# The values of the mLSTM mixer, split where they are made and stored as two parts

## The chip, the cores and the metric

One core of one Trainium2 chip runs the kernel. The metric is device time in microseconds of one launch, taken over several runs of the same program; the profile is one further execution of it. Every engine name is that of the profile: PE multiplies matrices, DVE, ACT and POOL work elementwise, SP and ACT issue the transfers of this kernel.

## The reference

One inference step of a trunk with two layers: a gMLP mixer (A) and an xLSTM mLSTM mixer (B), over 1024 frames of a prompt and 8 running streams of 16 frames each. All is fp32. What bears on the change is mixer B, for which the reference has, cut down:

```python
proj = xn @ w_in
xm, z = proj[..., :E], proj[..., E:]                  # E = 2048
xc = silu(causal_conv(xm))                            # 4 taps
q, k, v = blockdiag(xc, wq), blockdiag(xc, wk), blockdiag(xm, wv)
gates = concat(q, k, v) @ w_gates + b_gates           # ig, lf for each of 4 heads
# for each head (width 512) and chunk, with the state C (512 x 512) and n (512):
s   = (q @ k.T) * w_intra
num = s @ v + w_inter * (q @ C)
den = s.sum(-1) + w_inter * (q @ n)
h   = num / maximum(abs(den), exp(-m))
C   = decay * C + (w * k).T @ v
n   = decay * n + (w * k).sum(time)
# h: normalised per head, + skip * xc, * silu(z), @ w_out, + residual
```

The prompt starts from C = 0; each of the 8 sample streams has a state C for each head (1 MB each), which is read, updated and written back.

## The kernel before

The tokens stand in nine tiles of 128: eight of the prompt (n = 0 to 7) and one (n = 8) with the 8 x 16 sample frames. An fp32 product is made of three matmuls of rounded parts: `split` (L89, L90) gives a high part (a cast, on ACT) and a low part (source minus high part, on DVE, or on POOL where the call names `G`), and `mm3` multiplies high by high, high by low and low by high. All matmuls are issued by one wrapper (L58), so PE's rows in the profile all have that line and are told apart by their tiles. PE's order is that of a written list; the order of the other engines is made by a scheduler, and a tile that is given out again makes its next writer wait for its last reader.

The stages, with their place in the profiled execution: mixer A to about 840 us; the feature stage of mixer B (about 850 to 1145 us), 48 steps of some 6 us, one for each of 16 blocks of 128 features and 3 batches of 3 token tiles; the gates and the z projection (1145 to 1405 us), beside which the first sample streams begin; the loop over 32 units, one for each head h and prompt tile n, and 4 riders (the sample tile of each head), with 22 sample streams among them (1405 to 1945 us); a short tail.

In a feature step `values` multiplies the inputs of the batch by block-diagonal weights into a PSUM tile of 128 x 3 x 136, copies the 3 x 128 values to an SBUF tile `st` (ACT, L777), adds the other columns to the gates (DVE, L778) and stores `st` to the scratch tensor `vb_d` of the head (a transfer issued by ACT, L779). `st` has 5 buffers, which the skip product `sk` (L780 to L782) and the z steps (L857 to L859) use too. `keys` makes queries and keys and stores them to `q_d` and `k_d` (L798). The inputs of the next feature go through a convolution on DVE (L755, L758), a silu on ACT (L760) and a split of two halves (`xc`, L89 and L90).

At the end of the feature stage the gates are gathered (`rA`, DVE, L887), `bgc` and `m0T` (L892, L894) are loaded, and the states of the first sample streams (`c`, L1111, 512 KB a transfer) are requested on the same queue, SP's.

`load_qkv` (L1016 to L1042) loads what a unit needs by transfers on SP's queue: `qT`, `kT`, `sk`, `zz`, the values `vv` (256 KB, L1031) and the decay weights `cw` (L1037). In the loop `mask` adds `cw` to a mask into `dd` (DVE, L1211), `prep_k` and `prep_s` scale and split keys and scores, `prep_v` (L1240 to L1247) splits `vv` into `va`, the operand tile of the values, with the high part on ACT and the low part on POOL, `scale_q` (L1252) and `prep_q` do the same for the queries, and `settle` updates the state `Cst` (L1278) and splits it into `Ch` and `Cl`, whose low part is made in four pieces, some on DVE and some on POOL. `va` has three buffers that take turns; two more columns of each hold ones and zeros, set once. `numerator` and `update` use the parts of `va` as operands of PE. After the numerator come the normalising operations (L1318 to L1330), the gate products (L1361, L1363) and the output projection, whose sums are added to the residual on DVE (L1380).

A head's sample tile is prepared by the class `Dec`: `keys` turns the keys to tokens, weights them (`kw`, L1082), splits keys and values (L1084, L1085; the low parts on POOL) and stores six pieces of them to the scratch tensor `st_d` (L1088), from which each stream loads its operand `sk` (L1108); `normaliser` updates n by a matmul over 512 columns and an operation on 8 partitions (`nn`, L1097).

Of the kernel before, what the change touches and what calls it, by code (L numbers as in the profile page):

```python
# [8 lines left out]
F32 = mybir.dt.float32  # L9
# [61 lines left out]
def trunk_kernel(ctx: ExitStack, tc: tile.TileContext, ins: dict, outs: list):  # L71
# [56 lines left out]
    vb_d = [dram.tile([NT * P, DH], F32, name=f"vb_d{h}") for h in range(H)]  # L128
# [577 lines left out]
    class Feature:  # L706
# [60 lines left out]
        def values(self, b):  # L767
# [8 lines left out]
            st = bw.tile([P, 3, P], F32, name="st", bufs=5)  # L776
            A.copy(out=st, in_=pvv[:, :, :P])  # L777
            V.tensor_tensor(out=gtok[:, 3 * b:3 * b + 3], in0=gtok[:, 3 * b:3 * b + 3], in1=pvv[:, :, P:], op=ALU.add)  # L778
            A.dma_start(out=vb_d[h].rearrange("(n p) e -> p n e", p=P)[:, 3 * b:3 * b + 3, fs], in_=st)  # L779
            sk = bw.tile([P, BT], F32, name="st", bufs=5)  # L780
# [67 lines left out]
    def z_steps():  # L848
        for f in range(NF):
# [3 lines left out]
            for b in range(NB):  # L853
# [3 lines left out]
                st = zs.tile([P, BT], F32, name="st", bufs=5 if zs is bw else 2)  # L857
# [129 lines left out]
    dec8 = const.tile([SB, H], F32, name="dec8")  # L987
    selh = gt.tile([H, H, P], F32, name="selh")
    V.tensor_copy(out=selh, in_=ident[:H, :H].unsqueeze(2).to_broadcast([H, H, P]))
    tpd, tp8 = (ps.tile([P, DH], F32, name="sm") for _ in range(2))  # L990
    for h in range(H):
        T.matmul(tpd[:, 16 * h:16 * h + 16], selh[:, h], de16, start=True, stop=True)
    T.transpose(tp8[:SB, :H], de16[:, 8:16], ident[:H, :H])
    V.tensor_copy(out=decB.rearrange("p h c -> p (h c)"), in_=tpd[:, :16 * H])
    V.tensor_copy(out=dec8, in_=tp8[:SB, :H])
# [22 lines left out]
    def load_qkv(pool, h, n, want, prev=None, bufs=None):  # L1018
# [10 lines left out]
        if "v" in want:  # L1029
            t = pool.tile([P, DH], F32, name="vv")  # L1030
            l = S.dma_start(out=t, in_=vb_d[h][ts, :])  # L1031
            if prev is not None:
                after(l, prev)
            got["v"] = t
# [17 lines left out]
    class Dec:  # L1052


        def __init__(self, h, prev):
# [4 lines left out]
            kv = self.kv = rawp.tile([P, 2, DH], F32, name="raw")  # L1060
            loads = (S.dma_start(out=kv[:, 0].rearrange("p (c t) -> p c t", c=DC), in_=k_d[h].rearrange("(c p) t -> p c t", p=P)[:, :, 8 * P:]),
                     S.dma_start(out=kv[:, 1], in_=vb_d[h][8 * P:, :]))
# [3 lines left out]
            self.nn = dw.tile([SB, DH], F32, name="nn")  # L1066
            S.dma_start(out=self.nn, in_=ins["state_mlstm_n"][0, :, h])
# [5 lines left out]
        def keys(self):  # L1073
# [6 lines left out]
            kp = k_tokens(self.kv[:, 0].rearrange("p (c t) -> p c t", c=DC), ps, "sm")  # L1080
            kw = self.kw = rawp.tile([P, DH], F32, name="raw")
            A.activation(out=kw, in_=kp, func=AF.Copy, scale=tok[:, 8, 1, h:h + 1])  # L1082
            kv = wp.tile([P, 4, DH], F32R, name="w")
            split(kv[:, 0], kv[:, 1], kw, G)  # L1084
            split(kv[:, 2], kv[:, 3], self.kv[:, 1], G)  # L1085
            for r, (kpart, vpart) in enumerate(((0, 2), (0, 3), (1, 2))):
                for q, part in enumerate((kpart, vpart)):
                    S.dma_start(out=f32(st_d[h])[:, r * SL:(r + 1) * SL, q, :], in_=f32(kv)[:, part])  # L1088
# [499 lines left out]
```

## Time and profile before

| | us |
|---|---|
| runs (three) | 1966.57, 1967.85, 1975.25 |
| median | 1967.85 |
| profiled execution, its own time | 1961.52 |
| its span in the trace | 1959.8 |
| busy: PE | 1900.5 (97%) |
| busy: DVE | 1270.3 (65%) |
| busy: ACT | 850.0 (43%) |
| busy: POOL | 621.4 (32%) |
| DMA, mean over the span | 167 GB/s, 328.21 MB |

The profiled execution is 6.33 us below the median of the runs. In the views of the trace a busy time is the union of an engine's instructions; a wait is the idle time of an engine before an instruction, put down to what ended it; the chain is the work that ended last, followed back from the end; PEclk is the clock granted to PE, as a share of 2.4 GHz, so that 1.00 is the upper of its two levels and 0.50 the lower (1.2 GHz). DMA is the mean busy share of the 16 DMA engines.

### The profile page before, as it was taken

The numbers are of one execution on the slowest core, as the hardware profiler recorded it, in microseconds if no ns is written. First come the engines' busy times: TensorE is split into PE (matmuls) and PEld (weight loads), VectorE is DVE, ScalarE is ACT, GpSimd is POOL, SyncE is SP. The second block draws the span as 40 slices with busy tenths as digits, with TensorE's granted clock in tenths as the row PEclk, the third lists the DMA queues.
The fourth block names the chain that finished last, engine by engine and source line by source line (L and its number), as shares of the span: only waits on it lengthen the run. The fifth ranks groups of instructions, "written<-read, shape, count | busy, mean of one in ns | idle before, by whom it ended". The sixth has DMA issues, their size and how long they took to land.

```text
span 1959.8 us, 32037 instructions
## 1 busy us (share of the span) xinstructions
PE 1900.5 (97%) x11553; PEld 1681.2 (86%) x11553; DVE 1270.3 (65%) x2522; ACT 850.0 (43%) x1727; POOL 621.4 (32%) x637
## 2 busy tenths in 40 slices
PE   7999999999998999989999989999999999999998
PEld 6888999999998788889999959888987787788887
DVE  5822477777776354477667635222498798898897
ACT  5422444444444243455555635112343344344454
POOL 3000244444441000035444401000145435345466
PEclk9999999999999999999999979999999999999999
DMA  6222333333334654335555554687998897775533
GB/s 213 92 92 77 106 98 103 103 103 99 103 98 163 200 170 142 113 99 154 161 162 156 167 152 143 207 259 235 282 306 264 267 284 243 261 239 177 154 122 129
DMA packets 345690, 328.21 MB, mean 167 GB/s; under 512 B 28164, under 2 KB 276948, under 8 KB 345532
## 3 DMA queue, kind: packets, MB, share of 16 engines
q1 hardware_dynamic: 288812, 261.03, 43.3%
q10 hardware_dynamic: 56720, 65.13, 10.6%
q8 instruction: 91, 1.49, 0.3%
q14 instruction: 67, 0.55, 0.1%
HBM read 203.07 MB, written 123.02 MB: 166 GB/s over the span
## 4 chain that ended last, share of the span: by engine, by line
PE 74%; DVE 13%; DMA 7%; ACT 2%; issue 2%; POOL 1%; SPq 1%; ACTq 0%; POOLq 0%; DVEq 0%
PE sm L58 74%; DVE Cst L1278 2%; DMA cw<-cw_d 2%; DVE c L1129 2%; DVE Cl L90 1%; DVE qT L1252 1%; DMA out<-c 1%; DVE raw L1361 1%; DVE bst L1318 1%; DMA c<-in_state_mlstm_C 1%; DMA vv<-vb_d 1%; DMA r<-in_a_w_in 0%; DVE dn L1324 0%; DVE x L1380 0%; DMA st_d<-w 0%
## 5 line engine op out<-in xcount | busy, mean ns | idle before, releaser
L58 PE MATMUL sm<-xh,w 128*128 128x384 f32 x1536 | 410.9, 341 | 4.3 <-DVE w L90 1.5
L58 PEld LDWEIGHTS sm<-xh,w 128*128 128x128 f32 x1536 | 281.5, 189 | 12.8 <-issue 8.2
L58 PE MATMUL sm<-xl,w 128*128 128x384 f32 x768 | 260.4, 339 | 1.1 <-DVE xl L90 1.1
L58 PE MATMUL sm<-Xh,w 128*128 128x288 f32 x1024 | 216.3, 298 | 4.6 <-ACT c L499 4.6
L58 PE MATMUL sm<-w,o 128*128 128x512 f32 x864 | 209.9, 398 | 2.9 <-ACT o L89 1.2
L58 PE MATMUL sm<-w,os 128*128 128x512 f32 x864 | 200.7, 393 | 6.6 <-ACT os L89 6.6
L58 PEld LDWEIGHTS sm<-w,os 128*128 128x128 f32 x864 | 162.9, 190 | 42.8 <-ACT os L89 9.1
L58 PEld LDWEIGHTS sm<-w,o 128*128 128x128 f32 x864 | 159.8, 188 | 41.1 <-ACT hn L1330 1.7
L58 PE MATMUL sm<-w,Xh 128*128 128x512 f32 x576 | 180.2, 394 | 1.8 <-DVE w L90 1.4
L58 PEld LDWEIGHTS sm<-Xh,w 128*128 128x128 f32 x1024 | 168.2, 189 | 5.2 <-ACT c L499 5.0
L90 DVE TENSOR_TENSOR w<-r,w 128x512 fp32r<-128x512 f32 x176 | 136.1, 779 | 50.3 <-ACT w L89 49.8
L58 PE MATMUL sm<-S,w 128*128 128x288 f32 x1152 | 163.8, 297 | 0.0
L90 DVE TENSOR_TENSOR w<-raw,w 128x1024 fp32r<-128x1024 f32 x44 | 56.4, 1281 | 156.8 <-ACT w L89 156.7
L58 PEld LDWEIGHTS sm<-S,w 128*128 128x128 f32 x1152 | 155.1, 188 | 0.8
L58 PE MATMUL sm<-Xl,w 128*128 128x288 f32 x512 | 151.4, 296 | 0.0
L58 PEld LDWEIGHTS sm<-xl,w 128*128 128x128 f32 x768 | 145.1, 189 | 1.3 <-DVE xl L90 1.3
L89 ACT CAST w<-r 128x512 fp32r<-128x512 f32 x176 | 107.3, 618 | 68.8 <-PE sm L58 29.3
L58 PEld LDWEIGHTS sm<-w,Xh 128*128 128x128 f32 x576 | 108.0, 189 | 25.3 <-DVE w L90 2.6
L58 PE MATMUL sm<-w,Xl 128*128 128x512 f32 x288 | 112.6, 391 | 0.0
L90 DVE TENSOR_TENSOR os<-or,os 128x384 fp32r<-128x384 f32 x96 | 53.0, 556 | 90.1 <-ACT os L89 90.1
L58 PE MATMUL sm<-va,k 128*128 128x258 f32 (+1 forms) x768 | 104.5, 286 | 3.4 <-DVE x L1380 1.7
L89 ACT CAST w<-raw 128x1024 fp32r<-128x1024 f32 (+1 forms) x56 | 55.2, 987 | 116.6 <-DMA raw<-in_b_w_in 91.2
(306 smaller groups left out, 3734.5 us busy)
## 6 DMA issues: line engine op xcount, KB each, us to landing
c<-in_state_mlstm_C SPq DMA_DIRECT2D x64, 512.0 KB
out<-c SPq DMA_DIRECT2D x64, 512.0 KB
r<-in_a_w_in SPq DMA_DIRECT2D x96, 256.0 KB
or<-o_d SPq DMA_DIRECT2D x96, 192.0 KB
raw<-in_b_w_in SPq DMA_DIRECT2D x32, 512.0 KB
qT<-q_d SPq DMA_DIRECT2D x40, 256.0 KB
vh<-v_d SPq DMA_DIRECT2D x48, 192.0 KB
vb_d<-st ACTq DMA_DIRECT2D x48, 192.0 KB
```

Of the source, the lines that this page charges most:

```text
L58: ins = fn(*args, **kw)
L89: first = A.copy(out=hi, in_=src)
L90: (lo_eng or V).tensor_tensor(out=lo, in0=src, in1=f32(hi), op=ALU.subtract)
L1129: V.scalar_tensor_tensor(out=c0[:, cc], in0=c0[:, cc], scalar=decB[:, d.h, 8 + b:9 + b], in1=pc, op0=ALU.mult, op1=ALU.add)
L1252: V.tensor_tensor(out=u.g["qT"], in0=u.g["qT"], in1=u.g["cw"][:, 1:2].to_broadcast([P, DC, P]), op=ALU.mult)
L1278: V.scalar_tensor_tensor(out=Cst[:, c, a, :w], in0=Cst[:, c, a, :w], scalar=decB[:, h, n:n + 1], in1=pc, op0=ALU.mult, op1=ALU.add)
L1318: V.bn_stats(out=bst[:, a], in_=hn[:, a, :256])
L1361: V.scalar_tensor_tensor(out=og[:, c], in0=u.pT[:, c], scalar=colB[:, HNG, 4 * h + c:4 * h + c + 1], in1=g["sk"][:, c], op0=ALU.mult, op1= ...
```

## The change

1. `values`: the PSUM values are split at once into a tile `sv` of two parts (high part by ACT, low part by DVE) in place of the copy to `st`; two transfers, one a part, store them to `vb_d`, which now has two parts. `st` has 3 buffers in place of 5, `sv` has 2.
2. `load_qkv`: the values come by two transfers of 256 KB, one a part, straight into the next `va` tile; `vv` and `prep_v` are gone. `va` has four buffers in place of three. A written-down order of this load after an earlier instruction (`after`) is dropped.
3. `Dec`: keys and values of the sample tile have a tile each; the values arrive as two parts and go from there to `st_d`, without a split; the weighted keys are written over the keys' tile.
4. `normaliser`: n is kept transposed, and updated by four matmuls of 8 columns and two operations on 128 partitions; the last head transposes and stores it once for all. The loads `nn` and the small tile `dec8` are gone.

```diff
--- before.py
+++ after.py
@@ -125,7 +125,7 @@
     k_d = [dram.tile([DH, NT * P], F32, name=f"k_d{h}") for h in range(H)]
-    vb_d = [dram.tile([NT * P, DH], F32, name=f"vb_d{h}") for h in range(H)]
+    vb_d = [dram.tile([2, NT * P, DH], F32R, name=f"vb_d{h}") for h in range(H)]
     sk_d = [dram.tile([DH, NT * P], F32, name=f"sk_d{h}") for h in range(H)]
@@ -773,11 +773,12 @@
                 T.matmul(pvv[:, j], lhs, self.bdv, start=True, stop=True)
-            st = bw.tile([P, 3, P], F32, name="st", bufs=5)
-            A.copy(out=st, in_=pvv[:, :, :P])
+            sv = bw.tile([P, 2, 3, P], F32R, name="sv", bufs=2)
+            split(sv[:, 0], sv[:, 1], pvv[:, :, :P])
             V.tensor_tensor(out=gtok[:, 3 * b:3 * b + 3], in0=gtok[:, 3 * b:3 * b + 3], in1=pvv[:, :, P:], op=ALU.add)
-            A.dma_start(out=vb_d[h].rearrange("(n p) e -> p n e", p=P)[:, 3 * b:3 * b + 3, fs], in_=st)
-            sk = bw.tile([P, BT], F32, name="st", bufs=5)
+            for q in range(2):
+                A.dma_start(out=f32(vb_d[h])[q].rearrange("(n p) e -> p n e", p=P)[:, 3 * b:3 * b + 3, fs], in_=f32(sv)[:, q])
+            sk = bw.tile([P, BT], F32, name="st", bufs=3)
             G.tensor_scalar(out=sk, in0=self.xc[b], scalar1=colB[:, SKIP, f:f + 1], scalar2=None, op0=ALU.mult)
...
@@ -1027,11 +1025,10 @@
         if "v" in want:
-            t = pool.tile([P, DH], F32, name="vv")
-            l = S.dma_start(out=t, in_=vb_d[h][ts, :])
-            if prev is not None:
-                after(l, prev)
-            got["v"] = t
+            va = got["v"] = vas[0]
+            vas.append(vas.pop(0))
+            for q in range(2):
+                S.dma_start(out=f32(va)[:, q, :, :256], in_=f32(vb_d[h])[q, ts, :].rearrange("p (a e) -> p a e", a=2))
         if "cw" in want:
@@ -1057,14 +1054,13 @@
             self.ev = []
-            kv = self.kv = rawp.tile([P, 2, DH], F32, name="raw")
-            loads = (S.dma_start(out=kv[:, 0].rearrange("p (c t) -> p c t", c=DC), in_=k_d[h].rearrange("(c p) t -> p c t", p=P)[:, :, 8 * P:]),
-                     S.dma_start(out=kv[:, 1], in_=vb_d[h][8 * P:, :]))
+            self.kT = rawp.tile([P, DC, P], F32, name="raw")
+            self.vv = rawp.tile([P, 2, DH], F32, name="raw")
+            loads = (S.dma_start(out=self.kT, in_=k_d[h].rearrange("(c p) t -> p c t", p=P)[:, :, 8 * P:]),
+                     S.dma_start(out=self.vv, in_=f32(vb_d[h])[:, 8 * P:, :].rearrange("q p e -> p q e")))
             for l in loads:
                 if prev is not None:
                     after(l, prev)
-            self.nn = dw.tile([SB, DH], F32, name="nn")
-            S.dma_start(out=self.nn, in_=ins["state_mlstm_n"][0, :, h])
 
@@ -1077,25 +1073,32 @@
 
-            kp = k_tokens(self.kv[:, 0].rearrange("p (c t) -> p c t", c=DC), ps, "sm")
-            kw = self.kw = rawp.tile([P, DH], F32, name="raw")
+            kp = k_tokens(self.kT, ps, "sm")
+            kw = self.kw = self.kT.rearrange("p c t -> p (c t)")
             A.activation(out=kw, in_=kp, func=AF.Copy, scale=tok[:, 8, 1, h:h + 1])
-            kv = wp.tile([P, 4, DH], F32R, name="w")
+            kv = wp.tile([P, 2, DH], F32R, name="w")
             split(kv[:, 0], kv[:, 1], kw, G)
-            split(kv[:, 2], kv[:, 3], self.kv[:, 1], G)
-            for r, (kpart, vpart) in enumerate(((0, 2), (0, 3), (1, 2))):
-                for q, part in enumerate((kpart, vpart)):
-                    S.dma_start(out=f32(st_d[h])[:, r * SL:(r + 1) * SL, q, :], in_=f32(kv)[:, part])
+            for r, (kpart, vpart) in enumerate(((0, 0), (0, 1), (1, 0))):
+                for q, src in enumerate((f32(kv)[:, kpart], self.vv[:, vpart])):
+                    S.dma_start(out=f32(st_d[h])[:, r * SL:(r + 1) * SL, q, :], in_=src)
             dj = dw.tile([P, SB], F32, name="dj")
             V.tensor_tensor(out=dj, in0=pd[:, :SB], in1=blk8, op=ALU.mult)
             V.tensor_reduce(out=dint[:, h:h + 1], in_=dj, axis=mybir.AxisListType.X, op=ALU.add)
 
         def normaliser(self):
             h = self.h
-            pn = ps.tile([P, DH], F32, name="sm")
-            T.matmul(pn[:SB], blk8, self.kw, start=True, stop=True)
-            V.scalar_tensor_tensor(out=self.nn, in0=self.nn, scalar=dec8[:, h:h + 1], in1=pn[:SB], op0=ALU.mult, op1=ALU.add)
-            A.dma_start(out=n_s[0, :, h, :], in_=self.nn)
+            pn = ps.tile([P, DC, SB], F32, name="sm")
+            for c in range(DC):
+                T.matmul(pn[:, c], self.kw[:, c * P:(c + 1) * P], blk8, start=True, stop=True)
+            nv = n0T[:, :, :, h]
+            V.tensor_tensor(out=nv, in0=nv, in1=decB[:, h, 8:16].unsqueeze(1).to_broadcast([P, DC, SB]), op=ALU.mult)
+            V.tensor_tensor(out=nv, in0=nv, in1=pn, op=ALU.add)
+            if h == H - 1:
+                pt = ps.tile([P, P], F32, name="sm")
+                T.transpose(pt, n0T.rearrange("p c b h -> p (c b h)"), ident)
+                no = rawp.tile([P, P], F32, name="raw")
+                V.tensor_copy(out=no, in_=pt)
+                A.dma_start(out=n_s[0].rearrange("b h (c p) -> c (b h) p", p=P), in_=no)
 
@@ -1156,7 +1159,7 @@
     me = ctx.enter_context(tc.tile_pool(name="me", bufs=2, reuse_waits="tile"))
-    vas = [me.tile([P, 2, 2, VA], F32R, name=f"va{j}", bufs=1) for j in range(3)]
+    vas = [me.tile([P, 2, 2, VA], F32R, name=f"va{j}", bufs=1) for j in range(4)]
     for va in vas:
@@ -1237,15 +1240,6 @@
 
-    def prep_v(u):
-
-        if u is None:
-            return
-        va = u.va = vas[0]
-        vas.append(vas.pop(0))
-        vv = u.g["v"].rearrange("p (a e) -> p a e", a=2)
-        split(va[:, 0, :, :256], va[:, 1, :, :256], vv, G)
-
     def scale_q(u):
@@ -1271,7 +1265,7 @@
             for v in parts:
-                mm3(pc, v.k2[:, 0, cs], v.k2[:, 1, cs], v.va[:, 0, a, :w], v.va[:, 1, a, :w], v is parts[0], v is u)
+                mm3(pc, v.k2[:, 0, cs], v.k2[:, 1, cs], v.g["v"][:, 0, a, :w], v.g["v"][:, 1, a, :w], v is parts[0], v is u)
             if n == 1:
@@ -1280,13 +1274,13 @@
 
-        va = u.va
+        va = u.g["v"]
         o = u.num[a] = ps.tile([P, VA], F32, name="sm")
         w = VA - 2 * a
         o = o[:, :w]
         mm3(o, u.s2[:, 0], u.s2[:, 1], va[:, 0, a, :w], va[:, 1, a, :w], True, not u.inter and u.n != 1)
         if u.n == 1:
-            vb = u.before.va
+            vb = u.before.g["v"]
             mm3(o, u.sO[:, 0], u.sO[:, 1], vb[:, 0, a, :w], vb[:, 1, a, :w], False, True)
...
```

In the built program this moves instructions of POOL and SP. POOL in the loop, three units of the first head; `Cl` is the low part of the state, `q` that of the queries, `va` that of the values, and `dn` belongs to the normalising. Before:

```order
L90 TENSOR_TENSOR Cl<-Cst,Ch 128x514
L90 TENSOR_TENSOR q_17922<-qT,q_17922 128x512
L1326 TENSOR_TENSOR dn<-dn,mhalf 128x1
L90 TENSOR_TENSOR Cl<-Cst,Ch 128x514
L90 TENSOR_TENSOR va_12456<-vv,va_12456 128x2x256
L90 TENSOR_TENSOR Cl<-Cst,Ch 128x514
L1326 TENSOR_TENSOR dn<-dn,mhalf 128x1
L90 TENSOR_TENSOR q_18133<-qT,q_18133 128x512
L90 TENSOR_TENSOR Cl<-Cst,Ch 128x514
L90 TENSOR_TENSOR va_12457<-vv,va_12457 128x2x256
L90 TENSOR_TENSOR Cl<-Cst,Ch 128x514
```

After:

```order
L90 TENSOR_TENSOR q_17756<-qT,q_17756 128x512
L90 TENSOR_TENSOR Cl<-Cst,Ch 128x514 x2
L90 TENSOR_TENSOR q_17975<-qT,q_17975 128x512
L1320 TENSOR_TENSOR dn<-dn,mhalf 128x1
L90 TENSOR_TENSOR Cl<-Cst,Ch 128x514 x2
L1320 TENSOR_TENSOR dn<-dn,mhalf 128x1
L90 TENSOR_TENSOR q_18184<-qT,q_18184 128x512
L90 TENSOR_TENSOR Cl<-Cst,Ch 128x514 x2
```

Between the two `Cl` of a unit stood the `va`; now they follow each other.

SP at the end of the feature stage, with the semaphores of the first instruction. Before:

```order
L892 DMA bgc<-in_b_b_gates 4x2x1 [waits DMAHW6_49,DMAHW3_49,DMAHW7_49,DMAHW0_49,Activation_49]
```

After:

```order
L893 DMA bgc<-in_b_b_gates 4x2x1 [waits DMAHW3_49,DMAHW5_49,DMAHW2_49,DMAHW7_49,DMAHW1_49,Activation_49]
```

Among the transfers that `bgc` waits for there are now the last stores to `q_d` and `k_d`; before they were those of the step before. The loads `c` stand right behind on SP's queue in both. In the gates stage, where the first head's sample tile is prepared, SP has before (`w` is the tile of the split keys and values):

```order
L1031 DMA vv<-vb_d_102 128x512 x2
L1088 DMA st_d_128<-w 8x16x512 x3
L1031 DMA vv<-vb_d_102 128x512
L1088 DMA st_d_128<-w 8x16x512 x3
L1108 DMA sk_12626<-st_d_128 48x1024
```

After (`raw` holds the values as they were loaded):

```order
L1083 DMA st_d_128<-raw 8x16x512 x3
L1031 DMA va_12548<-vb_d_102 128x2x256 x2
L1031 DMA va_12549<-vb_d_102 128x2x256 x2
L1031 DMA va_12550<-vb_d_102 128x2x256 x2
L1034 DMA cw<-cw_d 128x2x128
L1023 DMA zz<-z_d_110 128x4x128
L1031 DMA va_12551<-vb_d_102 128x2x256 x2
L144 DMA raw<-in_b_w_in 128x8x128
L1083 DMA st_d_128<-w 8x16x512 x3
L1111 DMA sk_12721<-st_d_128 48x1024
```

The three stores of values go ahead of the loads of `va`; the three of keys alone stand before the load of `sk`. In a unit of the fourth head SP has before:

```order
L1111 DMA c_18466<-in_state_mlstm_C 128x2x512
L1111 DMA c_18468<-in_state_mlstm_C 128x2x512
L1025 DMA kT<-k_d_100 128x4x128
L1031 DMA vv<-vb_d_105 128x512
L1037 DMA cw<-cw_d 128x2x128
```

After:

```order
L1114 DMA c_18059<-in_state_mlstm_C 128x2x512
L1031 DMA va_12548<-vb_d_104 128x2x256
L1114 DMA c_18061<-in_state_mlstm_C 128x2x512
L1031 DMA va_12548<-vb_d_104 128x2x256
L1023 DMA kT<-k_d_100 128x4x128
L1034 DMA cw<-cw_d 128x2x128
```

One transfer of values between `kT` and `cw` has become two that stand ahead of `kT`.

## Rows read from the trace of the kernel before

**Rows 1.** Busy time by stretch: start:end, length, PE PEld DVE ACT POOL, PEclk, DMA, GB/s.

```profile
900.00:1100.00 200.00, 199.82 (x1205) 187.42 (x1204) 137.47 (x307) 118.09 (x262) 90.42 (x131) 1.00 0.57 161
1400.00:1500.00 100.00, 96.01 (x653) 77.18 (x651) 85.82 (x187) 45.43 (x90) 43.82 (x35) 0.99 0.93 286
1500.00:1900.00 400.00, 390.42 (x2559) 326.52 (x2556) 349.63 (x754) 177.08 (x341) 193.79 (x153) 0.99 0.71 224
```

**Rows 2.** Waits of PE over the span: total us, times, longest us.

```profile
PE sm L58 <- DVE x L1380: 8.3, 7, 2.7
PE sm L58 <- DVE rA L887: 7.5, 1, 7.5
...
PE sm L58 <- DMA sk<-st_d: 2.4, 1, 2.4
```

**Rows 3.** Chain of waits, 1140 to 1160 us: start us, us, what.

```profile
1146.88 2.00 DMA z_d<-st
...
1148.90 5.08 DMA c<-in_state_mlstm_C
...
1153.98 0.56 DVE rA L887
```

**Rows 4.** Timeline of ACT's transfers, 1140 to 1155 us: start us, us, instruction.

```profile
1141.85 0.38 ACTq L779 DMA_DIRECT2D vb_d<-st  x1
...
1148.45 0.61 ACTq L798 DMA_DIRECT2D k_d<-qk  x1
```

**Rows 5.** Timeline of SP, 1140 to 1156 us.

```profile
1147.99 6.17 SPq L1111 DMA_DIRECT2D c<-in_state_mlstm_C  x4
```

**Rows 6.** Chain of waits, 1210 to 1245 us.

```profile
1225.04 1.27 POOL w L90
...
1228.55 8.29 DMA st_d<-w
...
1236.95 3.27 DMA sk<-st_d
```

**Rows 7.** Busy time of two stretches of 20 us, columns as in rows 1.

```profile
1160.00:1180.00 20.00, 20.00 (x79) 11.78 (x79) 9.76 (x12) 6.34 (x6) 0.00 (x0) 0.67 0.09 21
1240.00:1260.00 20.00, 19.73 (x100) 17.69 (x101) 7.80 (x10) 5.04 (x8) 0.00 (x0) 0.91 0.76 241
```

**Rows 8.** Groups of instructions, 860 to 1140 us: count | busy us, mean ns | idle before.

```profile
L777 ACT COPY st<-sm 128x384 f32<-128x384 f32 x45 | 22.0, 489 | 1.1 <-PE sm L58 0.6
```

**Rows 9.** Groups of instructions over the whole span.

```profile
L90 DVE TENSOR_TENSOR os<-or,os 128x384 fp32r<-128x384 f32 x96 | 53.0, 556 | 90.1 <-ACT os L89 90.1
```

**Rows 10.** Timeline of DVE, 1015 to 1030 us: start us, us, instruction.

```profile
1015.45 0.55 DVE L90 TENSOR_TENSOR xc<-xc,xc 64x384 fp32r<-64x384 f32 x1
```

**Rows 11.** Timeline of PE in the same stretch.

```profile
1019.37 0.95 PE L58 MATMUL sm<-xc,bd 128*128 128x384 f32 x4
```

**Rows 12.** Groups of instructions, 1400 to 1945 us.

```profile
L90 POOL TENSOR_TENSOR va<-vv,va 128x512 fp32r<-128x512 f32 x33 | 42.4, 1289 | 18.7 <-ACT va L89 18.5
...
L90 DVE TENSOR_TENSOR Cl<-Cst,Ch 128x514 fp32r<-128x514 f32 x48 | 56.5, 1177 | 0.9 <-ACT Ch L89 0.8
...
L1211 DVE TENSOR_TENSOR dd<-cw,m_pr 128x128 f32<-128x128 f32 x30 | 8.7, 290 | 20.4 <-DMA cw<-cw_d 20.4
```

**Rows 13.** Timelines of DVE and of POOL, 1630 to 1636 us.

```profile
1632.97 0.70 DVE L90 TENSOR_TENSOR Cl<-Cst,Ch 128x514 fp32r<-128x514 f32 x1
...
1631.94 1.18 POOL L90 TENSOR_TENSOR va<-vv,va 128x512 fp32r<-128x512 f32 x1
```

**Rows 14.** The same, 1650 to 1658 us.

```profile
1652.92 1.62 DVE L90 TENSOR_TENSOR Cl<-Cst,Ch 128x514 fp32r<-128x514 f32 x1
...
1652.79 1.19 POOL L90 TENSOR_TENSOR va<-vv,va 128x512 fp32r<-128x512 f32 x1 [0.72 <-ACT va L89]
```

**Rows 15.** Chain of waits, 1484 to 1512 us.

```profile
1490.45 5.72 DMA cw<-cw_d
...
1496.55 0.61 DVE x L1380
```

More of the change, by code (lines that the diff above doesn't have):

```diff
@@ L856, in z_steps @@
                     last = done[NF + f] = mm3(pm, w[:, 0, k], w[:, 1, k], xh[b][:, k], xl[b][:, k], k == 0, k == KD - 1)
-                st = zs.tile([P, BT], F32, name="st", bufs=5 if zs is bw else 2)
+                st = zs.tile([P, BT], F32, name="st", bufs=3 if zs is bw else 2)
                 A.activation(out=st, in_=pm, func=AF.Silu)
@@ L986, in trunk_kernel @@
     decB = const.tile([P, H, 16], F32, name="decB")
-    dec8 = const.tile([SB, H], F32, name="dec8")
     selh = gt.tile([H, H, P], F32, name="selh")
     V.tensor_copy(out=selh, in_=ident[:H, :H].unsqueeze(2).to_broadcast([H, H, P]))
-    tpd, tp8 = (ps.tile([P, DH], F32, name="sm") for _ in range(2))
+    tpd = ps.tile([P, DH], F32, name="sm")
     for h in range(H):
         T.matmul(tpd[:, 16 * h:16 * h + 16], selh[:, h], de16, start=True, stop=True)
-    T.transpose(tp8[:SB, :H], de16[:, 8:16], ident[:H, :H])
     V.tensor_copy(out=decB.rearrange("p h c -> p (h c)"), in_=tpd[:, :16 * H])
-    V.tensor_copy(out=dec8, in_=tp8[:SB, :H])
     k0 = const.tile([P, H], F32, name="k0")
@@ L1446, in first_scores @@
         prep_s(u)
-        prep_v(u)
     plan.setdefault(last - 5, []).append(first_loads)
@@ L1493, in trunk_kernel @@
         scale_q(nxt)
-        prep_v(nxt)
         prep_q(nxt)
@@ L1500, in trunk_kernel @@
             prep_s(rid)
-            prep_v(rid)
         if rid1:
```

## Prediction

> **What bounds the kernel now.** I first read busy time by stretch. In the feature stage PE works 199.82 of 200 us [rows 1], so nothing that another engine gives up there can shorten it, and nothing that it takes on lengthens it until its slack is used up. In the loop, 1400 to 1900 us, PE is busy 96.01 and 390.42 us, so idle 3.99 + 9.58 = 13.6 us; the granted clock is 0.99, which is worth some 5 us more in 500. DVE is busy 85.82 + 349.63 of the 500 us, 87%, and is the next engine to bind. So the loop can give back at most 13.6 + 5 = 18.6 us, whatever the change takes off DVE, ACT or POOL.
>
> The waits of PE show where the idle time lies [rows 2]: 8.3 us in seven waits for the residual add on DVE, most of it the loop's; one of 7.5 us for `rA` at the gates; one of 2.4 us for a load from `st_d`. Other waits belong to mixer A and are untouched. I then followed the chain at the two single waits [rows 3, 6] and at a long wait in the loop [rows 15]. All sums are made against the profiled execution, 1961.52 us; the median of the runs is 1967.85, that is 6.33 more, and this is added at the end.
>
> **Feature stage.** Each of the 48 steps swaps the copy of 489 ns [rows 8] for a cast of the same elements, taken at the same price, and adds a subtraction on DVE and one more store issue on ACT. The subtraction has no row; the nearest is the one of 128 x 384 elements, 0.556 us [rows 9], whose source lies in SBUF and not in PSUM. The issue takes 0.38 us [rows 4]. Together 0.94 us a step. The cover is the distance from a step's inputs to their use: the second half of `xc` is split by 1015.45 + 0.55 = 1016.00 us [rows 10], and the matmuls that read it begin at 1019.37 [rows 11], 3.37 us later; this is the shortest of the distances that recur every three steps. 0.94 is below 3.37, and DVE has 200 - 137.47 us idle in 200 [rows 1], so it does not pile up. I take 0. Were the cover gone it would be 48 x 0.94 = 45 us. The added 9.4 MB of stores meet a DMA share of 0.57: nothing.
>
> **Gates.** `rA` is a copy on DVE that in the built program waits for the last stores of queries and keys. The last one was issued by 1148.45 + 0.61 = 1149.06 us [rows 4], while the four stream loads of 512 KB had been pushed from 1147.99 on [rows 5], and `rA` began at 1153.98. The chain names the loads (5.08 us) because they share the DMA engines. A store just ahead of them took 2.00 us [rows 3]. The order shown above now lets `bgc`, and with it the loads behind it on SP, start only when these stores have landed. So `rA` would start at 1149.06 + 2.00 = 1151.06, 2.9 us earlier. I take **-2.5**, since `bgc` itself then comes later; bounds 0 (the loads were not to blame) and -5.1 (all of that wait). The loads themselves come some 3 us later, behind which the z weights wait on SP; the stretch from 1160 moves only 21 GB/s [rows 7], so I cost it at nothing. PE still waits some 5 us, so the reduced clock behind it (0.67 [rows 7]) stays as it is.
>
> **The first head's sample tile.** The load from `st_d` waited for six stores, of which 8.29 us stand in the chain, then took 3.27 us [rows 6]. The split of the values on POOL, 1.27 us ahead of them, is gone; three of the six stores are issued early; the unit's `va` split that stood between the two is gone too. If half of the 8.29 us goes, the load is some 5 us earlier; PE had waited 2.4 us for it [rows 2]. So this wait vanishes. Behind it the clock was 0.91 in 20 us [rows 7], 1.8 us of work at the upper level. I take 2.4 + 1.8 = **-4.2**; bounds -4.2 and 0 (another operand of the stream is as late). PE waited only once for such a load [rows 2], so the three later heads count as 0.
>
> **The loop.** `prep_v` took 33 x 1.289 = 42.4 us of POOL [rows 12] and as many casts of ACT. Neither engine binds (POOL is busy 43.82 + 193.79 of 500 us [rows 1]), so their own time is worth nothing. What it does to DVE is worth something. The same low part of the state took DVE 0.70 us where POOL's `va` only covered its start [rows 13], and 1.62 us where a `va` of 1.19 us had begun just before it [rows 14]: 0.92 us more. Bounds: 0, if POOL's next operation, now moved up, meets DVE instead; and 33 x 0.92 = 30.4 us, if each of the 33 met such an operation. I take half, 15 us of DVE, since only DVE's operations with two inputs in SBUF show this.
>
> The Trainium skill, page "SBUF — State Buffer", section "SBUF: two separate sides", says that such an operation of DVE and one of GpSimd hold a shared pair of ports exclusively, so that the later one blocks for the whole of the earlier. Rows 14 agree: nearly all of `va` is found again in DVE's time. By that rule alone DVE could have lost up to the whole 42.4 us, and the loop would gain up to its ceiling.
>
> How much of the 15 us reaches PE? PE's own work fills 97% of the loop, and DVE's gain counts only where PE was waiting for DVE. I take half, **-8**; bounds 0 and the ceiling, -18.6.
>
> Against it stands the loads' side. Each unit reads 256 KB more; at the 286 GB/s of the fullest 100 us [rows 1] that is 0.92 us. DVE waited 20.4 us for `cw` over 30 units [rows 12], and one such wait held the residual add and so PE (5.72 us in the chain [rows 15]). `cw` used to come behind `kT` and `vv`; now both `va` loads stand ahead of `kT`, but they may start as soon as PE has read a tile of four loads earlier for the last time, so most of their bytes pass while SP still waits for the tile of `kT`. I take **+2**; bounds 0 and 0.92 x 11 = 10, were a third of the 30 units late by the full amount.
>
> **Normaliser.** One operation on 8 partitions less a head, two small ones and a final transpose more, and four small loads fewer on SP: 0, bounds -1 and +2 (the last head's store near the end).
>
> **Sum:** 0 - 2.5 - 4.2 - 8 + 2 = -12.7, so 1961.5 - 12.7 = 1948.8 us against the profiled execution, and 1955.2 on the scale of the median. A measurement of this kernel tells about 0.5% (9.8 us) from no change.
>
> **Rivals.**
> (A) *All of DVE's relief reaches PE.* For it: DVE's 87% and the waits of rows 2. Against: PE is already at 97%. -2.5 - 4.2 - 15 = -21.7: 1946.1.
> (B) *Only the two single waits go.* In the loop the two `Cl` of POOL now follow each other and meet DVE's operations just as `va` did, or DVE waits for `cw` instead. For it: 20.4 us of DVE's waits were for that load already. -6.7: 1961.2, which counts as no change.
> (C) *The transfers bind, and it gets slower.* If the DMA engines are full, each of the 33 added 256 KB delays `cw` and with it PE: 33 x 0.92 = 30.4, less 6.7, is +23.7: 1991.5. It decides from the point where the share reaches 1. In 1400 to 1500 it is 0.93, leaving 7 us, and six or seven units add 5.5 to 6.4; afterwards it is 0.71 [rows 1]. So the loads just fit, which speaks against it.
> (D) *The feature stage is bound by the chain of ACT and DVE.* +45 - 12.7: 2000.2. The 3.37 us of cover speak against it.
>
> **Chances.** My forecast 0.50, A 0.20, B 0.20, C 0.07, D 0.03. The range reaches from A with the loop's full ceiling (3.6 us below 1946.1, about 1942) to B with the full delay of `cw` (10 us, less what the gates may give, about 1969); it leaves out C, D and the outer ends. Faster by over 0.5% (below 1958.0): A and two thirds of my forecast, 0.54. Slower by over 0.5%: C and D, 0.10. The rest, 0.36, is within 0.5%.
>
> **What would show it.** Feature stage: PE still at 100%, steps of unchanged length; a wait of PE for `xc` would show (D). Gates: `rA` some 2 to 3 us earlier, the `c` loads issued behind the stores. First streams: no wait of PE for `sk<-st_d`, and no dip of the clock near 1240. Loop: the mean of DVE's `Cl` falls from 1.18 us [rows 12] towards 0.9, and PE's idle time falls by some 6 us. If `Cl` keeps its mean, (B) holds; if the wait for `cw` grows far above 20.4 us while the DMA share nears 1, (C) does. My forecast is wrong if the loop's length, from 1405 on, changes by less than 2 us or by more than 14.

## The result and the profile after

The changed kernel takes 1982.84 us (median of five runs, 1978.83 to 1983.81) against 1967.85 us: a ratio of 1.0066 with a 95% interval of 1.0048 to 1.0085, so 13 us slower (9 to 17); the two medians alone are 15.0 us apart. The forecast was 1955.2 us in a range of 1942 to 1969. Its sign is wrong. The profiled execution of the changed kernel took 1978.83 us, with a span of 1977.1.

To see where the time went I cut the trace at the starts of five matmuls that both kernels issue: the first of mixer B's inputs, the last one of queries and keys (end of the feature stage), the first transpose of `rA` (end of the gates' wait), the last one of the z projection, and the last one of the output projection (end of the loop). Later runs gave more profiles of the same programs, which stand beside the first (us):

| stage | before, 3 profiles | changed, 2 profiles | means differ by | forecast |
|---|---|---|---|---|
| features | 308.4, 308.7, 308.9 | 312.9, 313.7 | +4.6 | 0 |
| gates' wait | 7.9, 8.1, 8.7 | 5.5, 5.5 | -2.7 | -2.5 |
| z projection, first streams | 250.4, 249.0, 253.3 | 253.5, 256.3 | +4.0 | -4.2 |
| loop | 547.1, 551.8, 550.5 | 559.3, 563.7 | +11.7 | -6 |

The means add to 17.6 us; the second profiled execution of the changed kernel, 1988.47 us, was longer than its timed runs.

Busy time by stretch, changed kernel (columns as in [rows 1]):

```profile
840.00:1150.00 310.00, 307.70 (x1822) 285.99 (x1823) 234.63 (x520) 177.90 (x393) 123.04 (x198) 0.99 0.64 180
1405.00:1500.00 95.00, 92.02 (x631) 77.38 (x630) 79.84 (x178) 39.85 (x77) 31.83 (x26) 0.98 0.99 307
1500.00:1800.00 300.00, 281.76 (x1795) 229.37 (x1794) 236.90 (x533) 110.84 (x210) 104.23 (x83) 0.96 0.82 259
```

PE now idles 18.2 us between 1500 and 1800, at a mean clock of 0.96; before it idled 9.6 in the 400 us from 1500 [rows 1]. Over the whole loop, as cut for the table, PE idles 23.2 and 24.8 us in the two profiles of the changed kernel and 15.2, 17.6 and 17.7 us in those of before, 7.2 us more by the means; the other 4.5 us are longer busy time, at a mean clock of 0.98 and 0.97 where it was 0.99, 0.98 and 0.99. The DMA engines are at 0.99 in the first 95 us of the loop, where rows 1 had 0.93; but PE idles only 3.0 us there.

Waits of PE over the span, changed kernel, beside [rows 2]:

```profile
PE sm L58 <- DVE x L1374: 10.3, 5, 3.4
...
PE sm L58 <- ACT ev L1125: 6.0, 3, 2.7
PE sm L58 <- DVE rA L888: 5.2, 1, 5.2
...
PE sm L58 <- DVE n0T L1095: 2.4, 1, 2.4
PE sm L58 <- DMA sk<-st_d: 2.3, 1, 2.3
```

The wait for `rA` fell from 7.5 to 5.2 us as forecast. The wait for the load from `st_d` is where it was in the first profile of before; the other two of before had 0 and 1.2 us, the second one of the changed kernel 0.3. Groups of DVE's instructions from 1405 to 1965 us, the first answering to [rows 12]:

```profile
L90 DVE TENSOR_TENSOR Cl<-Cst,Ch 128x514 fp32r<-128x514 f32 x48 | 44.2, 922 | 0.6 <-ACT Ch L89 0.5
...
L1214 DVE TENSOR_TENSOR dd<-cw,m_pr 128x128 f32<-128x128 f32 x30 | 8.9, 297 | 41.1 <-DMA cw<-cw_d 41.1
```

DVE's part of the state fell from 1177 to 922 ns, which is what the forecast said of POOL's missing subtractions. But the wait for `cw` doubled, from 20.4 to 41.1 us (42.6 with the riders' `dd`, which the experiments quote). One place shows how. SP's timeline of the changed kernel, in the unit where the loop loses most:

```profile
1567.40 2.34 SPq L1114 DMA_DIRECT2D c<-in_state_mlstm_C  x2
1569.83 2.49 SPq L1031 DMA_DIRECT2D va<-vb_d  x4
1572.42 0.55 SPq L1023 DMA_DIRECT2D kT<-k_d  x1
1573.02 0.50 SPq L1034 DMA_DIRECT2D cw<-cw_d  x1
```

The same unit before:

```profile
1556.95 2.41 SPq L1111 DMA_DIRECT2D c<-in_state_mlstm_C  x2
1559.45 0.42 SPq L1025 DMA_DIRECT2D kT<-k_d  x1
1559.96 0.46 SPq L1031 DMA_DIRECT2D vv<-vb_d  x1
1561.67 0.36 SPq L1037 DMA_DIRECT2D cw<-cw_d  x1
```

The chain of waits of the changed kernel, and DVE's timeline there:

```profile
1573.02 6.45 DMA cw<-cw_d
...
1580.35 0.48 ACT ev L1125
...
1580.88 4.15 PE sm L58 x16
```

```profile
1579.56 0.29 DVE L1214 TENSOR_TENSOR dd<-cw,m_pr 128x128 f32<-128x128 f32 x1 [6.25 <-DMA cw<-cw_d]
```

Four value loads of 256 KB stood ahead of `cw`, two for each of two units, where one had stood. SP was held at the loads of `c` until 1569.74 and then issued them, `kT` and `cw` without a pause. The four took 2.49 us of SP's time, and `cw` then needed 6.45 us to land, behind 2.25 MB that had been issued in 5.6 us. Before, `cw` was there when DVE reached it: `dd` began at 1565.73, at most 4.1 us after the issue, with no wait. Of the six waits for `cw` of 4 us and more in this profile of the changed kernel, four came behind four value loads issued in a row or around one `kT`. The product's copies on ACT (`ev`) stand behind `dd`, which is why PE's waits name them too.

### The profile page after: what moved, and what is told of

It reads as the page before. It is cut to its first block, busy times and chain, and to the rows that moved or that the text cites. A ratio compares the mean times of both kernels' runs of the same rounds, so it can differ in the third digit from the quotient of the medians.

```text
span 1977.1 us, 32179 instructions
## 1 busy us (share of the span) xinstructions
PE 1910.7 (97%) x11577; PEld 1691.8 (86%) x11577; DVE 1274.9 (64%) x2577; ACT 830.5 (42%) x1687; POOL 556.9 (28%) x597
## 3 DMA queue, kind: packets, MB, share of 16 engines
q10 hardware_dynamic: 75988, 74.57, 12.3%
## 4 chain that ended last, share of the span: by engine, by line
PE 77%; DMA 9%; DVE 9%; issue 2%; ACT 2%; SPq 1%; POOL 1%; ACTq 0%; POOLq 0%; DVEq 0%
PE sm L58 77%; DMA out<-c 2%; DMA cw<-cw_d 2%; DMA raw<-in_b_w_in 1%; DVE c L1132 1%; DMA c<-in_state_mlstm_C 1%; DVE Cst L1272 1%; DMA sk<-st_d 1%; DVE Cl L90 0%; DMA x<-x_d 0%; DMA qT<-q_d 0%; DVE qT L1246 0%; DMA z_d<-st 0%; DVE raw L1355 0%; DMA raw<-vb_d 0%
## 5 line engine op out<-in xcount | busy, mean ns | idle before, releaser
L90 DVE TENSOR_TENSOR w<-r,w 128x512 fp32r<-128x512 f32 x176 | 136.0, 778 | 44.3 <-ACT w L89 43.7
L90 POOL TENSOR_TENSOR Cl<-Cst,Ch 128x514 fp32r<-128x514 f32 x48 | 69.9, 1456 | 126.5 <-ACT Ch L89 102.0
```

Source lines behind the costliest of these rows:

```text
L90: (lo_eng or V).tensor_tensor(out=lo, in0=src, in1=f32(hi), op=ALU.subtract)
```

## The experiments

All ratios are to the kernel before, in runs on the same chip. "cw ahead" is the first experiment, and the base of many others.

**1. cw ahead of the values.** In `load_qkv` the value loads go behind the load of `cw`:

```diff
-                S.dma_start(out=f32(va)[:, q, :, :256], in_=f32(vb_d[h])[q, ts, :].rearrange("p (a e) -> p a e", a=2))
...
+            cwl = l = S.dma_start(out=t, in_=cw_d[h, :, ts].partition_broadcast(P))
...
+                l = S.dma_start(out=f32(va)[:, q, :, :256], in_=f32(vb_d[h])[q, ts, :].rearrange("p (a e) -> p a e", a=2))
+                if "cw" in want:
+                    after(l, cwl)
```

> The changed kernel, but each unit's two value loads are ordered behind the unit's own load of cw on SP. Place theory (the two loads, standing ahead of kT and cw on one queue, hold cw back): DVE's wait for cw in the loop falls from 42.6 us to some 20, where it was before the change, the loop's 12 us of loss go, and the time is 1966 to 1972 us. Volume theory (the added bytes fill the DMA engines wherever they stand): the wait stays above 35 us and the time at 1979 to 1986.

Measured: 1967.17 us, 0.9991 (0.9974 to 1.0007): the whole loss is gone by the order of one queue. SP in the same unit, and DVE's group from 1405 to 1965 us:

```profile
1560.00 2.48 SPq L1116 DMA_DIRECT2D c<-in_state_mlstm_C  x2
1562.56 0.42 SPq L1023 DMA_DIRECT2D kT<-k_d  x1
1563.78 0.37 SPq L1029 DMA_DIRECT2D cw<-cw_d  x1
1564.20 1.18 SPq L1037 DMA_DIRECT2D va<-vb_d  x2
```

```profile
L90 DVE TENSOR_TENSOR Cl<-Cst,Ch 128x514 fp32r<-128x514 f32 x48 | 43.7, 911 | 0.5 <-ACT Ch L89 0.5
...
L1216 DVE TENSOR_TENSOR dd<-cw,m_pr 128x128 f32<-128x128 f32 x30 | 9.8, 325 | 28.1 <-DMA cw<-cw_d 28.1
```

The wait fell to 28.1, not to the 20 that the theory of the place had. DVE's part of the state is shorter than before, so DVE may reach `cw` earlier and turn part of its relief into waiting; that was not tested, and experiment 9 shows what else holds `cw` here.

**2, 3. Half the bytes,** in the changed kernel, and with cw ahead. The low part of the operand tile is zero in both, so the products with it are left out.

```diff
-            for q in range(2):
+            for q in range(1):
```

> The changed kernel, but the units load only the high part of the values; the low part of the operand tile is set to zero once, so the products with the low part of v are left out of the sums. The bytes of a unit's loads are those of before the change, and their place ahead of kT and cw stays. Volume theory: the wait for cw falls to 20 to 25 us, the time to 1966 to 1972. Place theory: the wait falls only in part, to 30 us or so, since one load still stands ahead, and the time to 1974 to 1979.

> The kernel with cw ahead of the value loads, and only the high part of the values is loaded by the units, the low part of the operand tile being zero, so the products with the low part of v are left out. It has the bytes of before and the place of the better order. If the added bytes cost something even behind cw, the loop gets 3 to 8 us shorter and the time is 1959 to 1964; if place alone mattered, the time stays at 1966 to 1968.

Measured: 1966.81 us, 0.9986 (0.9969 to 1.0003), and 1966.01, 0.9983 (0.9965 to 1.0002). By the time of the whole, halving what stands ahead of `cw` helps as much as moving all of it behind; halving what stands behind it shows nothing. By stages the first halving gives less: its loop took 549.3 us, some 6 us more than with cw ahead, and its z stage 249.3 us, where cw ahead has 254.7. In both views the added bytes cost only where `cw` waits for them. DVE's wait in the loop was 33.6 and 32.5 us. So neither theory of experiment 2 holds whole: the volume theory met the time but expected a wait of 20 to 25 us, the place theory came nearer to the wait (some 30 us) but expected a time of 1974 to 1979.

**4. Repeated profiles.** Programs of before (twice), changed and with cw ahead, unchanged.

> The kernel before, unchanged, for a second profile. If stages repeat, its loop is 547 us within 2 us, its feature stage 308.4 and its gates 7.9. If the loop is 550 us or more, the profile of before that the forecast was read from was a short one, and the loop with cw ahead is better by more than the first profiles show.

> The kernel before, unchanged, for a third profile: the same expectations as for the second.

> The changed kernel, unchanged, for a second profile. If the loss lies in the wait for cw, its loop is again 556 to 562 us and DVE's wait for cw there 38 us or more; if the first profile was a chance, the loop is near 550.

> The kernel with cw ahead of the value loads, for a second profile of the same program. By the forecast's net for the loop (6 us less than before) its loop is 540 to 545 us; if DVE's relief does not reach PE, it is as long as the loop of before in its new profiles.

Measured loops: before 551.8 and 550.5, so the forecast was read from a short one; changed 563.7, a little above what was expected, with a wait for `cw` of 44.0 us; cw ahead 544.5. By means, cw ahead has 543.4 us: 6.4 less than before (549.8) and 18.1 less than the changed kernel (561.5). The four kernels of experiments 8 and 10 have the loop of cw ahead too, the last one but for its first loads, and took 546.1 to 548.6 us; with them the mean is 545.8, 4.0 less than before and 15.7 less than the changed kernel.

**5. POOL's work put back,** in the kernel with cw ahead.

```diff
+        lo = u.g["v"][:, 1, :, :256]
+        G.tensor_tensor(out=lo, in0=f32(lo), in1=zeros[:, 0:1].unsqueeze(2).to_broadcast([P, 2, 256]), op=ALU.add)
```

> The kernel with cw ahead of the value loads, and POOL adds zero to the low part of each unit's values, where it subtracted before the change: the same engine, 128 x 512 elements, two inputs in SBUF; results do not change. By the forecast's step (POOL's subtraction stretched DVE by some 15 us, half of which reached PE) the mean of DVE's low part of the state rises from 0.92 us back to about 1.18, the loop gets 6 to 10 us longer and the time is 1973 to 1977. Full-relief rival: 12 to 18 us longer, 1979 to 1985. No-relief rival: DVE stretches, but PE does not wait for it: 1966 to 1970.

Measured: 1973.94 us, 1.0023 (1.0004 to 1.0042), inside the first range that was expected, but by luck: the mechanism did not come back. From 1405 us:

```profile
L90 DVE TENSOR_TENSOR Cl<-Cst,Ch 128x514 fp32r<-128x514 f32 x48 | 43.2, 900 | 0.5 <-ACT Ch L89 0.5
...
L1249 POOL TENSOR_TENSOR va<-va,zeros 128x512 fp32r<-128x512 f32 x33 | 36.6, 1108 | 79.9 <-DMA va<-vb_d 65.2 <-PE sm L58 9.1 <-DMA st_d<-w 5.3
```

DVE's part of the state stayed at 900 ns. POOL started these operations when the loads landed (65.2 us of its idle time before them ended so), and there they overlapped a `Cl` of DVE only 6 times, where `va` had done so 24 times before the change. The loop was 545.5 us in its one profile, which was the shortest execution of the ten, 1963.55 us; where the others lose is open. It does not tell the share of the relief that reaches PE.

**6. The old normaliser,** in the changed kernel and with cw ahead.

```diff
-            pn = ps.tile([P, DC, SB], F32, name="sm")
...
+            pn = ps.tile([P, DH], F32, name="sm")
+            T.matmul(pn[:SB], blk8, self.kw, start=True, stop=True)
...
```

> The changed kernel with the old normaliser: nn is loaded for each head, one matmul of 512 columns, one operation on 8 partitions. If the four small matmuls and two small operations put PE behind DVE and ACT (waits for n0T and ev, 7.5 us), those waits go and the time is 1973 to 1977. If they only showed a delay that came from cw, the waits move elsewhere and the time stays at 1980 to 1985.

> The kernel with cw ahead of the value loads, and with the old normaliser. If the new normaliser costs PE something by itself (its wait for n0T was still 2.0 us with cw ahead), the loop gets 2 to 7 us shorter and the time is 1960 to 1965. If its waits only passed on what the loads had delayed, the time stays at 1966 to 1969.

Measured: 1977.40 us, 1.0050 (1.0029 to 1.0071), whose interval overlaps that of the changed kernel, and 1969.31, 1.0005 (0.9985 to 1.0025), no better than with the new one. By the first time alone a cost of the normaliser is not shown. But the loop of that kernel took 552.1 us in its one profile, 9.4 less than the mean of the changed kernel, though DVE's wait for `cw` was still 39.0 us; with cw ahead the old normaliser has 544.7 us, no less than the new one. So the new normaliser may have a part in the loss where `cw` is late, and one profile does not settle it.

**7. The feature stage as before.**

```diff
-            split(sv[:, 0], sv[:, 1], pvv[:, :, :P])
+            A.copy(out=st, in_=pvv[:, :, :P])
...
-            for q in range(2):
-                A.dma_start(out=f32(vb_d[h])[q].rearrange("(n p) e -> p n e", p=P)[:, 3 * b:3 * b + 3, fs], in_=f32(sv)[:, q])
+            A.dma_start(out=vb_d[h].rearrange("(n p) e -> p n e", p=P)[:, 3 * b:3 * b + 3, fs], in_=st)
```

> The changed kernel with the feature stage of before: one copy and one store of the values in fp32, and both parts of the operand tiles are loaded from that one tensor, so v counts twice in place of its two parts. All loads of later stages keep their bytes and places. If the split and the second store cost the feature stage its 4.5 us, that stage ends 4.5 us earlier and the whole is at 1977 to 1980. If the 4.5 us come from elsewhere (the order of the first steps), nothing moves: 1981 to 1985.

Measured: the stage took 309.3 us, 3.6 to 4.4 less than in the changed kernel, so the split and the second store do cost it that. The whole stayed at 1982.01 us, 1.0062 (1.0042 to 1.0082): the gates' wait was 9.6 us where it had been 5.5. In this program `bgc` again waits for the stores of the step before, and SP had this:

```profile
1150.29 0.27 SPq L892 DMA_DIRECT2D bgc<-in_b_b_gates  x1
...
1151.49 6.30 SPq L1113 DMA_DIRECT2D c<-in_state_mlstm_C  x4
```

The stream loads were again pushed beside the last stores, and `rA` came at 1159.58, late by as much as the features were early. In the changed kernel `bgc` was issued at 1156.10 and the loads from 1157.30. This run shows the gates' step of the forecast from its other side. Its loop, with the loads of the changed kernel, took 561.5 us with 44.2 us of waiting for `cw`, so that loss repeats.

**8. Why the features are longer.** Six matmuls of 8 columns per feature sum the gates, two for each batch. PE before and in the changed kernel, the same feature:

```profile
1031.14 0.82 PE L58 MATMUL sm<-xc,gsum 128*8 128x384 f32 x6
```

```profile
1033.91 1.18 PE L58 MATMUL sm<-xc,gsum 128*8 128x384 f32 x6
```

Those of the three batches start together (within 0.34 us for all six) and run side by side. In the changed kernel those of batch 2 start late (0.69 us in 13 of 16 features), since they read its silu. ACT's timeline of the changed kernel, and DVE's, which ends the convolution:

```profile
1032.02 0.61 ACTq L780 DMA_DIRECT2D vb_d<-sv  x1
1033.32 0.48 ACT L745 COPY xmp<-sm 128x384 f32<-128x384 f32 x1 [2.63 <-DMA q_d<-qk]
1033.69 0.53 ACT L760 ACTIVATE xc<-xc 128x384 f32<-128x384 f32 x1
```

```profile
1032.34 0.34 DVE L758 SCALAR_TENSOR_TENSOR xc<-xms,colB,xc 128x128 f32<-128x128 f32 x1
```

The convolution is done at 1032.68; the silu stands behind the next step's copy and runs at 1033.69. Before, it began 0.04 us after its convolution:

```profile
1030.42 0.52 ACT L760 ACTIVATE xc<-xc 128x384 f32<-128x384 f32 x1 [2.20 <-DVE xc L758]
```

Three kernels tried to undo this, all with cw ahead: the low part behind the convolution on DVE; the silu ahead of the copy on ACT; both.

```diff
+            if b == 1 and self.conv is not None:
+                after(lo, self.conv)
```

```diff
+            if silu:
+                after(cp, silu[-1])
```

> The kernel with cw ahead of the value loads, and in the feature stage the low part of the values of batch 1 is subtracted behind the convolution of batch 2 on DVE, not in the middle of it. Theory: the subtraction delays the silu of batch 2, so that its gate matmul misses the other two, with which it would run side by side, once in each feature; then the stage of 838 to 1147 us gets 3 to 4.5 us shorter and the time is 1962 to 1965. Rival: the 4 us come from the second store or from ACT's waits for it; then the stage stays as long and the time at 1966 to 1969.

> The kernel with cw ahead of the value loads; in the feature stage each copy of a step's inputs (xmp) on ACT is ordered behind the silu of the step before. Theory: the split and the second store led to an order in which the silu of batch 2 stands behind the next step's copy, which waits for PE, so that its gate matmul starts some 0.35 us after the other two and the feature takes 18.43 us where it took 18.28; with the silu first, the six gate matmuls of a feature start within 0.34 us again, the stage of 838 to 1147 us gets 3 to 4 us shorter and the time is 1962 to 1967. Rival: the longer step comes from the added stores' traffic or from ACT's added work itself, and the stage keeps its 312 us and more: 1966 to 1970.

> The kernel with cw ahead of the value loads; in the feature stage the low part of batch 1 stands behind the convolution of batch 2 on DVE, and on ACT the silu of a step stands ahead of the next step's copy and of the store of that low part. The two runs that changed one of these orders alone made the stage longer, since the other engine's order then held the silu. Theory (the 4 us come from the late silu of batch 2): the six gate matmuls of a feature start within 0.34 us, the stage of 838 to 1147 us falls from 312.6 to some 309 us, and the time is 1962 to 1966. If it keeps 312 us and more with the matmuls together, the added work itself is the cause; if the matmuls still start apart, some other order holds the silu and the cause stays open.

Measured: 1973.20 us, 1.0020 (1.0004 to 1.0035); 1977.29, 1.0047 (1.0028 to 1.0065); 1973.06, 1.0026 (1.0008 to 1.0044). All three made the stage longer: 316.8, 320.5 and 319.1 us. Each order fixed by hand moved others; with the silu first, DVE put splits of the other batch between the parts of the convolution. The last one tells most: in seven of its features the gate matmuls start within 0.34 us, and from there to the next feature's it is 18.0 to 18.2 us; in six they start 1.75 to 2.47 us apart, and it is 19.4 to 20.1. In the changed kernel, at 0.69, it is 18.42 on average, before at 0.34 it is 18.19. So a feature gets longer by nearly what the last of these matmuls is late. In the changed kernel that makes 0.23 us in each of 15 steps, some 3.5 of the stage's 4.6 us; the rest is open. An order that cures all of them was not found.

**9. Three buffers for cw.** On top of the kernel with the silu first:

```diff
-            t = pool.tile([P, 2, P], F32, name="cw")
+            t = pool.tile([P, 2, P], F32, name="cw", bufs=None if pool is dw else 3)
```

> The kernel before this one in the list, with three buffers for cw (two before) and three for the operand tiles of the values (four before). If cw is late because its buffer comes free late, DVE's wait for it in the loop falls from some 30 us to below 15, the loop gets 3 to 8 us shorter, and the time is 1957 to 1964, below both kernels. If it is late because of what stands ahead of it on SP and in the DMA engines, the wait stays above 25 us and the time within 3 us of the kernel before this one; with one operand tile less it may also be up to 5 us longer.

Measured: 1970.71 us, 1.0002 (0.9990 to 1.0014), 6.6 us below the kernel it was built on, with three operand tiles in place of four. DVE's longest waits from 1405 us, in the kernel with the silu first and in this one:

```profile
DVE dd L1219 <- DMA cw<-cw_d: 31.2, 14, 4.6
DVE x L1379 <- PE sm L58: 25.4, 20, 2.2
```

```profile
DVE x L1379 <- PE sm L58: 35.4, 27, 2.9
DVE w L90 <- ACT w L89: 20.1, 8, 4.2
```

DVE's wait for `cw` is gone altogether. So what was left of it with cw ahead came, it seems, from the two buffers of `cw`. SP's rows under experiment 1 show such a pause: `kT` was issued by 1562.98 and `cw` from 1563.78, 0.8 us later, where the changed kernel had 0.05 us between them. The operand tile that went at the same time was not tested by itself. But PE gets little of it: it idles 16.4 us in the loop in place of 16.9, and the loop takes 544.2 us in place of 547.0. DVE now waits longer for PE and for ACT. The loop is within the spread of the others with cw ahead (542.2 to 548.6), and this profile, 1975.00 us, is the longest execution of the twelve, so it does not show the gain in its place. The kernel is not faster than before.

**10. The first value loads behind the weight loads.**

```diff
+                after(l, w_last[0])
```

> The kernel with cw ahead of the value loads; the first units' eight value loads, which stood on SP in the gates stage ahead of a weight load of the z projection (issued 1223 us), are ordered behind the last of these weight loads. Theory: the late weight load held ACT and with it the weighted keys of the first head, so that PE waited 1.7 to 2.3 us for the load from st_d and some more behind it; then the weight load is issued some 5 us earlier, that wait goes, the stretch from the gates to the end of the z projection falls from 254.7 to 249 to 252 us, and the time is 1962 to 1966. Rival: the stores of the raw values to st_d, which wait for their own load to land, hold the queue just as long; then the weight load is issued at 1218 or later and the stretch stays at 254 to 256.

Measured: 1965.53 us, 0.9995 (0.9982 to 1.0008). PE's waits from 1150 to 1300 us in the changed kernel and in this one:

```profile
PE sm L58 <- DVE rA L888: 5.2, 1, 5.2
PE sm L58 <- DMA sk<-st_d: 2.3, 1, 2.3
PE sm L58 <- ACT raw L1078: 0.9, 1, 0.9
```

```profile
PE sm L58 <- DVE rA L891: 5.2, 1, 5.2
```

The wait for `st_d` is gone: the value loads, eight in the changed kernel and six with cw ahead, which the scheduler issues as soon as tiles are free, held the weight load and with it ACT and the keys. SP issued that weight load at 1219.43, not at 1223.16 as with cw ahead. Counted from the first transpose of `rA`, PE is 3.4 us ahead of the first profile with cw ahead by 1254 us; a later wait for `ev` (4.0 us, there 3.0) leaves 2.3 of it, so the stage took 252.5 us against 254.7, just above what was expected. That length alone proves nothing, since the other kernels with cw ahead and all value loads took 249.5 to 255.6 us for it.

## Why the prediction was wrong

**Gates: right.** -2.5 forecast, -2.7 by the means, and the run with the features as before shows the cause.

**DVE's relief: right in kind, and in size as far as DVE goes.** Rows 12 had 56.5 us for DVE's part of the state; it is 44.2 now, and 43.7 with cw ahead: 12.3 us less, where 15 were forecast for all of DVE. The rule of the Trainium skill that was cited ("SBUF — State Buffer", section "SBUF: two separate sides") agrees: with POOL's subtractions gone, the operation that they blocked is 0.26 us shorter on average. With cw ahead the loop is 6.4 us shorter than before by the first means and 4.0 by all six profiles, where the forecast's net was -6; that the first figure meets it is chance. How much of the relief reaches PE, -8 in the forecast, is not known: the run meant for it did not bring the collisions back.

**The loads' side: this step failed.** The forecast put +2 (at most +10) on 256 KB more per unit, and let most of these bytes pass "while SP still waits for the tile of `kT`". In the place shown they did not: SP stood at the loads of `c`, and behind them the value loads of two units, four transfers and 1 MB, left at once and stood ahead of `cw` both on SP and in the DMA engines. Putting `cw` ahead of them is worth 15.7 to 18.1 us of the loop (561.5 less 545.8 or 543.4), with the new normaliser perhaps taking part in the loss. The bound was worked out from the bytes that one unit adds, not from all that can stand ahead of one `cw`.

This is the sign that rival (C) gave, a longer wait for `cw` behind added bytes, but not its reason. The transfers as a whole do not bind: the same bytes behind `cw` cost nothing that shows. Nor did it need a DMA share of 1. In the first 95 us of the loop the share is 0.99 and PE hardly idles; between 1500 and 1800 it is 0.82 on average, and there the loop loses most. While DVE waits in the place shown, from 1573 to 1580 us, it is 0.95.

**First sample tile: failed.** -4.2 forecast, +4.0 by the means. The stores were issued early as the order showed; but the forecast did not price the eight value loads that the same order put ahead of the next weight load. The run that moves them takes PE's wait for `st_d` away, and so does the one with half the bytes; that they cause the whole +4.0 is not shown. The 2.4 us that were to vanish were in part a chance of one profile: the other two of before had 0 and 1.2 us.

**Features: failed.** 0 forecast, +4.6 found. The cover of 3.37 us was read at the wrong reader: the matmuls of queries and keys do have it, the gate matmuls, which read the silu itself, had 0.2 us (the silu before ends at 1030.94, they start at 1031.14). The busy share of PE hid it, since matmuls that run one after the other, not side by side, count as busy. It is rival (D) in kind, the chain of ACT and DVE, at a tenth of its price.

With the load order put right, these two stages eat up what the loop and the gates give: 0.9991. No kernel of this study is shown to be faster than the one before. In the prediction's chances, 0.20 and two thirds of 0.50 make 0.53, not 0.54; nothing hangs on it.

## What to carry to other kernels

A load that becomes wait-free and larger is issued earlier and all at once; look at which small, late load (here `cw`) now stands behind it on the same queue, and price all that can be ahead of it, not what one step adds. A wait on an engine that does not bind is no measure of the loss: three buffers for `cw` took 31.2 us of DVE's waiting away and 0.5 us of PE's. Before calling work covered, find every reader of what it delays, the one with the least slack first; a busy share of 100% does not show that PE has lost nothing.

## What was not expected of the hardware

Matmuls with 8 columns of weights ran three at a time, one of each batch, their outputs 32 partitions apart: the six of a feature took 0.82 us where one takes 0.49, and 1.18 us when the last pair came some 0.35 us late. The same program also spread more than thought: the loop of before took 547.1 to 551.8 us in three profiles, so a step of 6 us cannot be read from one profile of each kernel.
